# A hybrid Hyena and attention block on one core: plain float32 transforms, contiguous short convolutions, and gate projections placed inside the long convolutions

## The chip, the cores and the metric

The kernel runs on one core of one Trainium2 chip. The core has five engines with a queue of their own each: TensorE (PE; its weight loads are listed as PEld), VectorE (DVE), ScalarE (ACT), GpSimd (POOL) and SyncE (SP, which here only issues DMAs). The metric is the device time of one launch in microseconds. The kernel before took 1945.61 us (median of 3 runs, 1942.84 to 1947.03).

## The reference

One transformer block in float32, 1024 tokens of width 1024, 256 context tokens. A modulated norm of x is projected by one matrix `w_in`. Its first 1536 columns go through the Hyena branch, the next 1536 are queries, keys and values of a differential attention, and the last 2048 are two gates.

```python
h = modulate(rmsnorm(x, g_mix_pre), sh1, sc1)
proj = h @ w_in
y_hy = hyena_branch(proj[..., :1536], ...) @ w_hy_up
...  # rope, diff_attention over own and context keys and values, y_att
g_hy, g_att = split(sigmoid(proj[..., 3072:]), 2)
mixed = (g_hy * y_hy + g_att * y_att) @ w_out
x = x + g1 * rmsnorm(mixed, g_mix_post)
...  # swiglu and its residual

def short_conv(u, w, b):
    up = pad(u, ((0, 0), (1, 1), (0, 0)))
    return up[:, :L] * w[0] + up[:, 1:L + 1] * w[1] + up[:, 2:] * w[2] + b

def fftconv(u, hk, dbias):
    y = irfft(rfft(u, n=2 * L) * hk, n=2 * L)[:, :L]
    return y + u * dbias

def hyena_branch(u, ...):
    parts = split(short_conv(u, conv_w, conv_b), 3)
    z = parts[0]
    for n in range(2):
        z = parts[n + 1] * fftconv(z, hk[:, n], dbias[n])
    return z
```

The filters `hk` are spectra of sequences that a small sine network makes.

## The kernel before

All tiles have 128 partitions. Channels or features lie on partitions, and tokens along a row. One program is written in Python; a tile layer then gives each engine its instructions in an order of its own, by the priority in which they are written and by what its model of the engines says is ready. So the order on an engine is not the order of the text, and it is shown below where it matters. Each engine works strictly in its order.

Float32 products are mostly made as three products in a rounded form (float32r): `whi` times `h_hi`, `wlo` times `h_hi` and `whi` times `h_lo`, where `lo` is what rounding took from `hi`. A rounding is a cast on ACT, the rest a subtraction on DVE.

The stages up to attention:
- **Filters** (`filter_begin` to `filter_end`, four pairs of order `o` and channel half `c`). `make(r)` makes one of eight residues of the filter, `spec(r)` transforms it by products with the matrix `mfs`, and `dft8_even`, `dft8_odd` combine residues on DVE. The spectra go to DRAM (`kspec`). In the same time h is normed and split, and the first tiles of `w_in` are projected (`raw_tile`).
- **A projection tile** (`raw_tile`): load 128 columns of `w_in` (`wraw`), cast (`whi`), subtract (`wlo`), 48 products of 512 columns on PE (two halves of `whi` x8, `wlo` x8, `h_lo` x8), copy to SBUF (`gt`), store to `praw` or `graw`. `wraw`, `whi` and `wlo` have two buffers each.
- **Long convolutions** (`fftconv`, four calls). Forward: per residue pair four transposes on PE, a split (`uh`, `ul`), twelve products with a matrix that is loaded and cast anew each time (`matrix`, tiles `mr`, `mt`), sums from PSUM. Then a chain on DVE: `dft8_even`, product with the spectrum (`times_k`), `dft8_odd`, `times_k`, four sums, and `dft8_even`, `dft8_odd` again. `split` rounds the result (`Hh`, `Hl`); `finish` makes the inverse products, copies (`yt`), transposes back and multiplies into `p`, the other operand of the gate `parts[n + 1]`. The operands `u` and `p` come from `hyena_conv`, the short convolution, which reads and writes with a stride of 8 words, so that residues lie together.
- Around the convolutions `raws` projects the remaining ten tiles of the Hyena part.
- **Gates**: 16 tiles (`graw`), written after the context's statistics (`csq`, `rstd_bc`, `cx`, `c_hi`, `c_lo`), then Q, K and V of head 0, each 48 products, and the context's keys and values (`ctx_k`, `ctx_v`).
- **Attention**, mixing and the feed-forward follow.

Of the kernel before, what the change touches and what calls it, by code (L numbers as in the profile page):

```python
# [9 lines left out]
F32 = mybir.dt.float32  # L10
# [7 lines left out]
P = 128  # L18
# [8 lines left out]
NQUAD, NPAIR, NGEN = 4, 4, 4  # L27
# [4 lines left out]
NMR, NMT = 2, 2  # L32
# [32 lines left out]
def block_kernel(tc, xT, ctxT, cvec, cT, wada1, wada, vecs, lamv, dbias, zT, fw1, fw2, fv, fw3, decay, mfs, mis, rope,  # L65
# [13 lines left out]
    LOENG, M2ENG, HLENG = V, V, V  # L79
# [153 lines left out]
    def dft8_even(S, sign, out):  # L233
        t02, t13 = pair(), pair()
        tt(t02, S[:, 0::2], S[:, 1::2], ALU.add)
        tt(t13, S[:, 0::2], S[:, 1::2], ALU.subtract)
        tt(out[:, 0], t02[:, 0], t02[:, 1], ALU.add)
        tt(out[:, 1], t02[:, 0], t02[:, 1], ALU.subtract)
        pm_i(out[:, 2], t13[:, 0], t13[:, 1], sign)
        pm_i(out[:, 3], t13[:, 0], t13[:, 1], -sign)  # L240

    def dft8_odd(D, sign, out, d3neg=False):
# [24 lines left out]
    mft = fl.tile([P, 4, 1024], F32R, name="mft")  # L267
    mfn = fl.tile([P, 8, 2, P], F32R, name="mfn")
# [77 lines left out]

    def load_mf():
        for r in (0, 2, 1, 3):
            raw = wp.tile([P, 1024], F32, tag="wraw", bufs=2, name="mraw")
            nc.sync.dma_start(out=raw, in_=mfs[r])  # L350
            (A.copy if r % 2 == 0 else G.tensor_copy)(out=mft[:, r], in_=raw)
        for j in range(2):
            m5 = mft.rearrange("p a (j h q m) -> p j a h q m", j=2, h=2, q=2)
            ts(mfn[:, 4 * j:4 * j + 4], f(m5[:, j, :, :, 1]), -1.0, None, ALU.mult, ALU.bypass, G)

    def mfm(part, r):

        if part == 2:
            return mfn[:, r, 0], mfn[:, r, 1]
        c0 = r // 4 * 512 + part * P  # L360
        return mft[:, r % 4, c0:c0 + P], mft[:, r % 4, c0 + 256:c0 + 256 + P]
# [3 lines left out]
    def filter_spec(o, c):  # L365
# [12 lines left out]
        def make(r):  # L378
# [6 lines left out]
            x = fp.tile([P, 512], F32, tag="xb", bufs=2, name="gx")  # L385
# [137 lines left out]
    def hyena_conv(m, dst):  # L523
# [5 lines left out]
        v = lambda k: raw[:, k:k + L].rearrange("p (a r) -> p r a", r=8)  # L529
# [974 lines left out]
```

## Time and profile before

| | |
|---|---|
| runs shown, median | 1945.61 us |
| profiled execution | 1944.66 us, of which its span is 1942.9 us |
| PE busy | 1738.5 us (89% of the span) |
| DVE busy | 1466.7 us (75%) |
| ACT busy | 847.5 us (44%) |
| POOL busy | 72.3 us (4%) |
| mean granted clock of PE | 0.943 of full |
| DMA | 293.95 MB, 151 GB/s over the span |

A busy share is an average over stages with different limits, so the stages are to be read one by one. PE's products are pipelined: the duration of one is longer than the distance from one to the next, and the distance is what counts in a stream. A name such as `ps<-h_hi,whi` gives what an instruction writes and reads.

### The profile page before, as it was taken

The page shows a single profiled execution, that of the slowest core. Times are in us where ns is not written, and L with a number is a line of the kernel's source. Part 1 is how long each engine was busy: PE and PEld are TensorE (multiplying, and loading weights), DVE is VectorE, ACT ScalarE, POOL GpSimd, SP SyncE. Part 2 cuts the span into 40 slices and gives each one's busy share as a digit, 9 for nine tenths or more (in the row PEclk, how much of TensorE's full clock was granted, in tenths as well). Part 3 has the DMA queues.
Part 4 walks back from the last instruction along what each step waited for, and adds up shares of the span by engine and source line. Part 5 has one row for each costly group of instructions (what it writes and reads, how often), then busy time and mean ns, then how long its engine had stood idle before and what let it go on. Part 6 is the DMA issues. An engine that isn't in the chain of part 4 may idle for free.

```text
span 1942.9 us, 23060 instructions
## 1 busy us (share of the span) xinstructions
PE 1738.5 (89%) x8158; PEld 1395.7 (72%) x8158; DVE 1466.7 (75%) x2606; ACT 847.5 (44%) x1306; POOL 72.3 (4%) x72
## 2 busy tenths in 40 slices
PE   7999859567789999999999997889999999798996
PEld 3588647456678888888787775668888888586874
DVE  5898798886946348989885868787776657868667
ACT  4533425334242237666675634453333334444421
POOL 1000000000000121112000000000000000000001
PEclk9899969697989999999999998989999999898998
DMA  9244615234366374443725674322325222434384
GB/s 337 69 171 153 214 58 195 98 129 151 115 251 211 115 218 122 129 135 109 236 90 193 219 241 159 134 85 99 112 104 167 92 76 76 147 104 152 128 302 154
DMA packets 130659, 293.95 MB, mean 151 GB/s; under 512 B 14659, under 2 KB 35919, under 8 KB 129264
## 3 DMA queue, kind: packets, MB, share of 16 engines
q1 hardware_dynamic: 124320, 284.82, 43.1%
q10 hardware_dynamic: 6224, 7.66, 1.3%
q8 instruction: 64, 1.05, 0.2%
q14 instruction: 51, 0.42, 0.1%
HBM read 216.93 MB, written 75.50 MB: 151 GB/s over the span
## 4 chain that ended last, share of the span: by engine, by line
PE 62%; DVE 21%; DMA 8%; ACT 3%; issue 3%; SPq 1%; DVEq 0%; ACTq 0%
PE pj L1151 24%; PE ps L140 22%; DVE pair L83 4%; PE S L840 3%; DVE quad L83 3%; PE psf L408 2%; DVE u L86 2%; PE pt L862 2%; PE psf L614 1%; DMA mr<-mfs 1%; DVE wlo L83 1%; DMA dacc_t<-dacc 1%; PE pv L871 1%; DMA cv<-praw 1%; PE pv L873 1%
## 5 line engine op out<-in xcount | busy, mean ns | idle before, releaser
L83 DVE TENSOR_TENSOR wlo<-wraw,whi 128x512 fp32r<-128x512 f32 (+2 forms) x199 | 167.4, 850 | 94.0 <-ACT whi L132 72.7
L140 PE MATMUL ps<-h_hi,wlo 128*128 128x512 f32 x640 | 179.7, 408 | 3.0 <-DVE wlo L83 3.0
L1151 PE MATMUL pj<-hfc,whi 128*128 128x512 f32 x720 | 178.7, 390 | 0.0
L140 PE MATMUL ps<-h_hi,whi 128*128 128x512 f32 x640 | 171.9, 399 | 3.1 <-ACT h_hi L453 1.9
L140 PE MATMUL ps<-h_lo,whi 128*128 128x512 f32 x640 | 171.4, 394 | 0.0
L1151 PEld LDWEIGHTS pj<-hfc,whi 128*128 128x128 f32 x720 | 135.3, 188 | 28.7
L140 PEld LDWEIGHTS ps<-h_hi,wlo 128*128 128x128 f32 x640 | 121.8, 195 | 27.6 <-DVE wlo L83 4.5
L140 PEld LDWEIGHTS ps<-h_hi,whi 128*128 128x128 f32 x640 | 119.5, 191 | 28.0 <-ACT h_hi L453 3.8
L1151 PE MATMUL pj<-hfb,whi 128*128 128x512 f32 x480 | 127.5, 410 | 11.8 <-ACT whi L1143 11.8
L140 PEld LDWEIGHTS ps<-h_lo,whi 128*128 128x128 f32 x640 | 118.9, 190 | 22.9
L1151 PE MATMUL pj<-hfa,whi 128*128 128x512 f32 x480 | 121.6, 396 | 3.3 <-ACT whi L1143 3.3
L1143 ACT CAST whi<-wraw 128x512 fp32r<-128x512 f32 x120 | 72.4, 621 | 114.3 <-PE pj L1151 84.8
L1151 PEld LDWEIGHTS pj<-hfb,whi 128*128 128x128 f32 x480 | 94.0, 197 | 36.1 <-ACT whi L1143 13.4
L1143 ACT CAST whi<-s 128x512 fp32r<-128x512 f32 x90 | 54.5, 620 | 139.9 <-DVE s L83 89.8
L132 ACT CAST whi<-wraw 128x1024 fp32r<-128x1024 f32 (+2 forms) x94 | 88.2, 940 | 55.3 <-PE ps L140 33.8
L840 PE MATMUL S<-KS,Q 128*128 128x512 f32 (+1 forms) x384 | 107.6, 374 | 2.8 <-DVE pr L844 2.4
L1151 PEld LDWEIGHTS pj<-hfa,whi 128*128 128x128 f32 x480 | 90.8, 190 | 25.2 <-ACT whi L1143 4.4
L1151 PE MATMUL pj<-hfc,wlo 128*128 128x512 f32 x360 | 97.1, 392 | 5.3 <-DVE wlo L83 5.3
L614 PE MATMUL psf<-Hh,mt 128*128 128x256 f32 x128 | 37.2, 389 | 71.8 <-ACT Hh L597 71.8
L501 ACT COPY gt<-ps 128x512 f32<-128x512 f32 x56 | 32.7, 587 | 132.4 <-PE ps L140 88.1
L614 PEld LDWEIGHTS psf<-Hh,mt 128*128 128x128 f32 x128 | 29.3, 280 | 75.5 <-ACT Hh L597 75.2
L1151 PEld LDWEIGHTS pj<-hfc,wlo 128*128 128x128 f32 x360 | 67.3, 188 | 20.9 <-DVE wlo L83 7.0
(486 smaller groups left out, 3803.2 us busy)
## 6 DMA issues: line engine op xcount, KB each, us to landing
wraw<-win SPq DMA_DIRECT2D x46, 512.0 KB, 3.6
wada_t<-wada SPq DMA_DIRECT2D x32, 512.0 KB, 5.4
wraw<-wgate SPq DMA_DIRECT2D x28, 512.0 KB, 3.2
wraw<-wupf SPq DMA_DIRECT2D x28, 512.0 KB, 3.7
araw<-ad SPq DMA_DIRECT2D x44, 256.0 KB, 4.2
w_ada<-wada SPq DMA_DIRECT2D x16, 512.0 KB, 6.3
kspec<-quad SPq DMA_DIRECT2D x8, 1024.0 KB, 3.9
mr<-mfs SPq DMA_DIRECT2D x32, 256.0 KB, 3.7
```

Source lines behind the costliest of these rows:

```text
L83: (eng or V).tensor_tensor(out=out, in0=a, in1=b, op=op)
L86: V.scalar_tensor_tensor(out=out, in0=a, scalar=s, in1=b, op0=op0, op1=op1)
L132: A.copy(out=hi, in_=raw)
L140: T.matmul(out=ps, lhsT=w[:, k * P:(k + 1) * P], rhs=xs[k][j], start=start and i == 0, stop=stop and i == len(seq) - 1)
L408: T.matmul(out=out, lhsT=a, rhs=b, start=i == 0, stop=i == len(ops) - 1)
L501: A.copy(out=gt, in_=ps)
L614: T.matmul(out=po, lhsT=a, rhs=b, start=i == 0, stop=i == len(ops) - 1)
L840: T.matmul(out=S[:, :cn], lhsT=Q[j][:, i, qt * P:(qt + 1) * P], rhs=KS[i][:, c0:c0 + cn], start=j == 0, stop=j == 1)
L862: T.transpose(out=pt[:, b * 256 + qt * P:b * 256 + (qt + 1) * P], in_=av[qt][:, kt * P:(kt + 1) * P], identity=ident)
L871: T.matmul(out=pv[:, :256], lhsT=VH[:, kt], rhs=ah[:, xs], start=kt == 0, stop=False)
L1143: A.copy(out=hi, in_=src)
L1151: T.matmul(out=ps, lhsT=w[a][:, k * P:(k + 1) * P], rhs=xs[k][b], start=i == 0, stop=i == 11)
```

## The change

It has five parts.

1. The transforms by matrices (`spec`, and forward and inverse products in `fftconv`) become plain float32 products, one where there were three. The splits of their operands go (`ghi`, `glo`, `uh`, `ul`, `Hh`, `Hl`). The two halves of the matrices are added up once into `mf` and `mi`, which stay in SBUF; `matrix` and its loads and casts go.
2. The short convolution reads and writes without a stride. The transposes and the product into `p` read with the stride of 8 words in its place; `hyena_out` needs none.
3. The two calls of `pm_i` with opposite signs become one with operands of twice the width.
4. The remaining eight tiles of the Hyena part and the 16 gates' tiles are written inside `fftconv` by `filler`, six in each call. The loop over gates after the context's statistics goes.
5. Buffers: the filter's residues take one buffer of eight; `hk` has 3 buffers, `ut` 2.

```diff
@@ pm_i, dft8_even, dft8_odd
     def pm_i(out, a, b, sign):
-        o1, o2 = (ALU.subtract, ALU.add) if sign > 0 else (ALU.add, ALU.subtract)
-        tt(out[:, RE], a[:, RE], b[:, IM], o1)
-        tt(out[:, IM], a[:, IM], b[:, RE], o2)
+        minus, plus = (ALU.subtract, ALU.add) if sign > 0 else (ALU.add, ALU.subtract)
+        o = out.rearrange("p s (q c) -> p (s q) c", q=2)
+        a2, b2 = [v.rearrange("p (q c) -> p q c", q=2) for v in (a, b)]
+        tt(o[:, 0::3], a2, b2[:, ::-1], minus)
+        tt(o[:, 1:3], a2[:, ::-1], b2, plus)
...
-        pm_i(out[:, 2], t13[:, 0], t13[:, 1], sign)
-        pm_i(out[:, 3], t13[:, 0], t13[:, 1], -sign)
+        pm_i(out[:, 2:4], t13[:, 0], t13[:, 1], sign)
...
+    def matrices(dst, src, tile):
+        d5 = dst.rearrange("p (j r) q m -> p j r (q m)", j=2)
+        for r in (0, 2, 1, 3):
+            raw = tile()
+            nc.sync.dma_start(out=raw, in_=src[r])
+            r4 = raw.rearrange("p (j h x) -> p j h x", j=2, h=2)
+            tt(d5[:, :, r], r4[:, :, 0], r4[:, :, 1], ALU.add)
...
@@ filter_spec
-            hi = fg.tile([P, 512], F32R, tag="ghi", bufs=NGEN, name="ghi")
-            lo = fg.tile([P, 512], F32R, tag="glo", bufs=NGEN, name="glo")
-            A.copy(out=hi, in_=x)
-            tt(lo, x, f(hi), ALU.subtract, LOENG)
-            gen[r] = (hi, lo)
+            gen[r] = x
...
+                T.matmul(out=out, lhsT=mfm(part, r), rhs=gen[r][:, 0:256], start=True, stop=False)
+                T.matmul(out=out, lhsT=mfm(pb, rb), rhs=gen[rb][:, 256:512], start=False, stop=True)
@@ hyena_conv
-        v = lambda k: raw[:, k:k + L].rearrange("p (a r) -> p r a", r=8)
+        v = lambda k: raw[:, k:k + L]
@@ fftconv
-    def fftconv(u, o, c, p):
+    mi = yp.tile([P, 8, 2, P], F32, name="mi")
+    matrices(mi, mis, lambda: yp.tile([P, 1024], F32, tag="hk", bufs=NHK, name="mraw"))
+
+    def fftconv(u, o, c, p, filler):
+        by_r = lambda t: t.rearrange("p h (a r) -> p h r a", r=8)
...
-                    T.transpose(out=pt[:, j * 256 + h * P:j * 256 + (h + 1) * P], in_=u[:, h, rr], identity=ident)
-            uh = yp.tile([P, 512], F32R, tag="uh", bufs=2, name="uh")
-            ul = yp.tile([P, 512], F32R, tag="ul", bufs=2, name="ul")
-            A.copy(out=uh, in_=pt)
-            tt(ul, pt, f(uh), ALU.subtract)
+                    T.transpose(out=pt[:, j * 256 + h * P:j * 256 + (h + 1) * P], in_=by_r(u)[:, h, rr], identity=ident)
+            ut = yp.tile([P, 512], F32, tag="ut", bufs=NUT, name="ut")
+            A.copy(out=ut, in_=pt)
...
-                    T.matmul(out=po, lhsT=mh, rhs=uh[:, xs], start=True, stop=False)
-                    T.matmul(out=po, lhsT=ml, rhs=uh[:, xs], start=False, stop=False)
-                    T.matmul(out=po, lhsT=mh, rhs=ul[:, xs], start=False, stop=True)
+                    T.matmul(out=ps[:, part * 256:(part + 1) * 256], lhsT=mf[:, r + 4 * j, part],
+                             rhs=ut[:, j * 256:(j + 1) * 256], start=True, stop=True)
             sd_from_psum(pp[0], pp[1], S, D_, SLOT[r])
+            if r in (2, 3):
+                filler()
...
         times_k(Ze, 0)
+        filler()
...
         times_k(Zo, 1)
+        filler()
...
-            pv = p[:, :, r:r + 5:4, :]
+            pv = by_r(p)[:, :, r:r + 5:4, :]
             tt(pv, pv, pq.rearrange("p (h j a) -> p h j a", h=2, j=2), ALU.mult)
...
-        finish(0, split(H[:, 0:2]))
-        finish(2, split(H[:, 2:4]))
+        finish(0, [H[:, 0], H[:, 1]])
+        finish(2, [H[:, 2], H[:, 3]])
+        filler()
...
-        finish(3, [h53[1], h17[1]])
+        finish(3, [H[:, 3], H[:, 1]])
+        filler()
...
+    tiles = [(m, praw[m]) for m in (2, 3, 6, 7, 8, 9, 10, 11)] + [(24 + j, graw[j]) for j in range(NGT)]
+
+    def filler():
+        raw_tile(*tiles.pop(0))
...
-    fftconv(u0, 0, 0, p00)
-    raws(2, 3, 6, 7)
+    fftconv(u0, 0, 0, p00, filler)
...
-    for j in range(NGT):
-        raw_tile(24 + j, graw[j])
```

How the orders differ at three places follows. In each row stand the line, the operation, what it writes and reads, the size and how many in a row.

PE in the kernel before, second long convolution, from its last forward product (`ul`, `mt`) to its first inverse ones (`Hh`, `mt`):

```order
L564 MATMUL psf<-ul,mt 128x256
L140 MATMUL ps<-h_hi,whi 128x512 x8
L140 MATMUL ps<-h_hi,wlo 128x512 x8
L140 MATMUL ps<-h_lo,whi 128x512 x8
...
L140 MATMUL ps<-h_hi,whi 128x512 x16
L614 MATMUL psf<-Hh,mt 128x256 x2
L614 MATMUL psf<-Hl,mt 128x256
...
L620 MATMUL psf<-ident,yt 128x128 x4
```

PE in the changed kernel at the same place; `ut`, `mf` are operands of the forward products, `quad`, `mi` of the inverse ones:

```order
L543 MATMUL psf<-ut,mf 128x256 x4
L140 MATMUL ps<-h_hi,wlo 128x512 x8
L140 MATMUL ps<-h_lo,whi 128x512 x8
L140 MATMUL ps<-h_hi,whi 128x512 x8
...
L140 MATMUL ps<-h_hi,whi 128x512 x16
L582 MATMUL psf<-quad,mi 128x256 x4
L589 MATMUL psf<-ident,yt 128x128 x4
L582 MATMUL psf<-quad,mi 128x256 x4
L140 MATMUL ps<-h_hi,wlo 128x512 x4
```

Between the two sets of transform products stand 88 projection products before and 152 now (135 in the first convolution), and more of them stand between the inverse products.

PE in the kernel before, the end of the second Q/K tile, the context's keys (`c_hi`, `c_lo`) and the first V tile; the product `bc` of the context's norm lies some hundred products ahead, among the gates:

```order
L140 MATMUL ps<-h_hi,whi 128x512 x8
L184 MATMUL bc<-dg,ones 128x256
...
L140 MATMUL ps<-h_lo,whi 128x512 x8
L140 MATMUL ps<-c_hi,whi 128x256 x8
L140 MATMUL ps<-c_hi,wlo 128x256 x8
L140 MATMUL ps<-c_lo,whi 128x256 x8
L140 MATMUL ps<-h_hi,whi 128x512 x8
L140 MATMUL ps<-h_hi,wlo 128x512 x8
```

PE in the changed kernel, the second half of the second Q/K tile and what follows it:

```order
L170 MATMUL ss<-ones,csq 128x1 x2
L140 MATMUL ps<-h_hi,whi 128x512 x5
L140 MATMUL ps<-h_hi,wlo 128x512 x8
L140 MATMUL ps<-h_lo,whi 128x512 x8
L184 MATMUL bc<-dg,ones 128x256
L140 MATMUL ps<-c_hi,whi 128x256 x3
L140 MATMUL ps<-h_hi,whi 128x512 x3
...
L140 MATMUL ps<-c_hi,wlo 128x256 x8
L140 MATMUL ps<-c_lo,whi 128x256 x8
L140 MATMUL ps<-h_hi,wlo 128x512 x8
```

The sums of squares and `bc` have moved from among the gates to within and right behind the second Q/K tile, next to the products that need them. From the last row on, the two orders of PE are the same.

DVE in the kernel before, at the end of the small steps that lead to `dg`, the operand of `bc`; `wada_t` is the reduction in `ada_tile`:

```order
L86 SCALAR_TENSOR_TENSOR rs_q<-rs_q,rs 128x2
L83 TENSOR_TENSOR mcol<-vec,cols 128x8
L86 SCALAR_TENSOR_TENSOR rs<-rs_q,rs 128x2
L89 TENSOR_SCALAR dg<-ident,rs 128x128 x2
L151 ISA wada_t,cols<-wada_t,sc_3856,vec 128x1024
L151 ISA cols 128x1
L83 TENSOR_TENSOR cx<-cx,bc 128x2048
```

DVE in the changed kernel, from the shuffle of the second Q/K tile's second half (`sw<-ps`) on:

```order
L712 STREAM_SHUFFLE sw<-ps 128x512
L83 TENSOR_TENSOR rs_q<-rs,rs_m 128x2
L83 TENSOR_TENSOR t_4006<-ps,rp 128x512
L86 SCALAR_TENSOR_TENSOR rs_q<-rs_q,rs 128x2
L83 TENSOR_TENSOR sw<-sw,rp 128x512
L86 SCALAR_TENSOR_TENSOR rs<-rs_q,rs 128x2
L151 ISA wada_t,cols<-wada_t,sc_3796,vec 128x1024
...
L89 TENSOR_SCALAR dg<-ident,rs 128x128 x2
...
L83 TENSOR_TENSOR cx<-cx,bc 128x2048
```

The steps to `dg` now stand among the rope steps of the Q/K tiles, behind a shuffle that reads what PE has just made.

## Rows read from the trace of the kernel before

**Rows 1.** The page: PE and its granted clock in 40 slices, in tenths.
```profile
PE   7999859567789999999999997889999999798996
...
PEclk9899969697989999999999998989999999898998
```

**Rows 2.** Windows: from:to length, PE, PEld, DVE, ACT, POOL busy, clock, DMA.
```profile
79.00:184.00 105.00, 104.34 (x573) 90.62 (x574) 92.92 (x151) 40.38 (x60) 0.00 (x0) 0.96 0.36 128
184.00:233.00 49.00, 39.46 (x190) 31.38 (x189) 36.70 (x42) 23.61 (x28) 0.52 (x8) 0.97 0.68 232
...
320.40:358.50 38.10, 19.99 (x90) 16.21 (x88) 37.44 (x51) 8.74 (x10) 0.00 (x0) 0.81 0.20 70
358.50:406.00 47.50, 38.31 (x192) 31.56 (x193) 33.96 (x39) 26.20 (x37) 0.26 (x4) 0.80 0.58 194
...
556.00:647.50 91.50, 85.27 (x369) 70.01 (x368) 42.16 (x82) 23.96 (x36) 0.00 (x0) 0.96 0.64 229
```

**Rows 3.** Waits of PE, 184 to 648 us: total, times, longest.
```profile
PE psf L614 <- ACT Hh L597: 71.8, 9, 19.1
```

**Rows 4.** Timeline of PE: start, length, line, operation, count [idle before].
```profile
336.57 3.79 PE L140 MATMUL ps<-h_hi,whi 128*128 128x512 f32 x16
358.46 0.80 PE L614 MATMUL psf<-Hh,mt 128*128 128x256 f32 x2 [18.11 <-ACT Hh L597]
```

**Rows 5.** Timeline of PE, a stretch of projections, first and last group.
```profile
645.69 1.98 PE L140 MATMUL ps<-h_lo,whi 128*128 128x512 f32 x8
...
667.45 1.98 PE L140 MATMUL ps<-h_lo,whi 128*128 128x512 f32 x8
```

**Rows 6.** Timeline of PE, split products of 256 columns in a row.
```profile
231.75 0.28 PE L563 MATMUL psf<-uh,mt 128*128 128x256 f32 x1
...
232.94 0.28 PE L564 MATMUL psf<-ul,mt 128*128 128x256 f32 x1
```

**Rows 7.** Plain float32 products: timeline, and line 184 (least, median, most ns).
```profile
59.92 6.17 PE L294 MATMUL ada_ps<-w_ada,csil 128*2 128x512 f32 x14
66.02 1.98 PE L441 MATMUL bc<-dg,ones 128*128 128x512 f32 x4
...
L184 PE MATMUL bc<-dg,ones x14: 379/592/1220, 594.4 to 1930.3; 128*128 128x512 f32 x12, 128*128 128x256 f32 x2
```

**Rows 8.** Groups of DVE, 184 to 560 us: count, busy, mean ns, idle before.
```profile
L86 DVE SCALAR_TENSOR_TENSOR u<-cv,vec,u 128x1024 f32<-128x1024 f32 x24 | 52.4, 2184 | 14.1 <-ACT u L92 8.5 <-issue 5.2
...
L86 DVE SCALAR_TENSOR_TENSOR quad<-pair 128x1024 f32<-128x1024 f32 x18 | 21.2, 1220 | 0.0
...
L83 DVE TENSOR_TENSOR pair<-pair 128x256 f32<-128x256 f32 x36 | 12.8, 420 | 0.0
...
L83 DVE TENSOR_TENSOR u<-u,psf 128x512 f32<-128x512 f32 x16 | 11.0, 688 | 16.7 <-PE psf L620 16.7
```

**Rows 9.** Timeline of DVE, its chain between forward and inverse products: first, last.
```profile
322.27 2.35 DVE L83 TENSOR_TENSOR pair<-quad 128x1024 f32<-128x1024 f32 x2
...
358.60 1.21 DVE L83 TENSOR_TENSOR Hl<-quad,Hh 128x1024 fp32r<-128x1024 f32 x1
```

**Rows 10.** The context's preparation: chain, timelines, a tile's row, PE's first V tile.
```profile
558.78 8.13 DMA zs<-zlo
...
567.01 0.36 ACTq L773 DMA_DIRECT2D cx<-ctxT  x1
...
574.12 1.91 ACT L92 ACTIVATE csq<-cx 128x2048 f32<-128x2048 f32 x1 [5.56 <-DMA cx<-ctxT]
...
L151 DVE CUSTOM_DVE_ANT_0 wada_t<-wada_t,sc,vec x16: 1271/1276/1285, 578.6 to 612.4; 128x1024 f32<-128x1024 f32 x16
...
595.42 2.28 DVE L83 TENSOR_TENSOR cx<-cx,bc 128x2048 f32<-128x2048 f32 x1
...
673.96 1.98 PE L140 MATMUL ps<-h_hi,wlo 128*128 128x512 f32 x8
```

**Rows 11.** Loads of the transposes' stationary operand (least, median, most ns).
```profile
L548 PEld LDWEIGHTS psf<-ident,u x64: 137/140/143, 201.3 to 485.4; 128*128 128x128 f32 x64
```

More of the change, by code (lines that the diff above doesn't have):

```diff
@@ L345, in load_x @@
             nc.sync.dma_start(out=xk[k], in_=xT[k])
-    def load_mf():
[L348 to L354, printed above, removed]
+    def matrices(dst, src, tile):
[5 more added lines that the diff above has]
+            tt(d5[:, :, r], r4[:, :, 0], r4[:, :, 1], ALU.add)
+    def load_mf():
+        matrices(mf, mfs, lambda: wp.tile([P, 1024], F32, tag="wraw", bufs=2, name="mraw"))
+        act(mfn, mf[:, :, 1], AF.Copy, scale=-1.0)
     def mfm(part, r):
[L358 to L361, printed above, removed]
+        return mfn[:, r] if part == 2 else mf[:, r, part]
     fg = fstk.enter_context(pool("fgen", side="right"))
@@ L591, in fftconv @@
         tt(D_[:, 2:4], Zo[:, 0:2], Zo[:, 2:4], ALU.subtract)
-        def split(x):
-            hi = yp.tile([P, 2, 512], F32R, tag="hk", bufs=4, name="Hh")
-            lo = yp.tile([P, 2, 512], F32R, tag="hk", bufs=4, name="Hl")
-            A.copy(out=hi, in_=x)
-            tt(lo, x, f(hi), ALU.subtract, HLENG)
-            return [(hi[:, i], lo[:, i]) for i in range(2)]
         def finish(r, Hs):
@@ L603, in finish @@
             for j in range(2):
-                hi, lo = Hs[j]
-                po = ps[:, j * 256:(j + 1) * 256]
-                ops = []
-                m = matrix(mis[r, :, j * 512:(j + 1) * 512])
                 for part in range(2):
-                    mh = m[:, part * P:(part + 1) * P]
-                    ml = m[:, 256 + part * P:256 + (part + 1) * P]
-                    cs = slice(part * 256, (part + 1) * 256)
-                    ops += [(mh, hi[:, cs]), (ml, hi[:, cs]), (mh, lo[:, cs])]
-                for i, (a, b) in enumerate(ops):
-                    T.matmul(out=po, lhsT=a, rhs=b, start=i == 0, stop=i == len(ops) - 1)
+                    T.matmul(out=ps[:, j * 256:(j + 1) * 256], lhsT=mi[:, r + 4 * j, part],
+                             rhs=Hs[j][:, part * 256:(part + 1) * 256], start=part == 0, stop=part == 1)
             yt = fp.tile([P, 512], F32, tag="xb", bufs=2, name="yt")
@@ L645, in part @@
     def part(o, c):
[L646 removed]
+        p = yp.tile([P, 2, L], F32, tag="u", bufs=3, name="u")
         for h in range(2):
@@ L657, in block_kernel @@
     p00 = part(1, 0)
-    fftconv(u0, 0, 0, p00)
-    raws(2, 3, 6, 7)
+    fftconv(u0, 0, 0, p00, filler)
     u1 = part(0, 1)
     p01 = part(1, 1)
-    fftconv(u1, 0, 1, p01)
-    raws(8, 9, 10, 11)
+    fftconv(u1, 0, 1, p01, filler)
     p10 = part(2, 0)
-    fftconv(p00, 1, 0, p10)
+    fftconv(p00, 1, 0, p10, filler)
     hyena_out(0, p10)
     p11 = part(2, 1)
-    fftconv(p01, 1, 1, p11)
+    fftconv(p01, 1, 1, p11, filler)
     hyena_out(1, p11)
+    while tiles:
+        filler()
     hy.close()
```

53 lines of the change are left out of this document (14 added, 39 removed).

## The prediction

> **What bounds the kernel now.** I began with the page: its forty slices [rows 1] show TensorE (PE) at nine tenths or more nearly everywhere, except in the fifth to twelfth slice (about 195 to 585 us), where it stands at 5 to 9 and the granted clock at 6 to 9 tenths. There lie the long convolutions and the start of the gates' projections. Cutting the span at the stages [rows 2] shows two engines that take turns. Up to 184 us (filters) PE is busy 104.3 of 105.0. Between the last forward product of the second long convolution (320.4) and its first inverse one (358.5) VectorE (DVE) is busy 37.4 of 38.1 and PE 20.0. From there to 406 PE has 38.3 of 47.5 and DVE 34.0, at a granted clock of 0.80. In the gates (556 to 647.5) PE has 85.3 of 91.5 and DVE 42.2. The waits say on what PE stands: 71.8 us in nine waits for `Hh`, the rounded result of DVE's transform [rows 3]. In the timeline [rows 4] it runs out of projections after `whi` x16 at 336.57 and starts the inverse products 18.11 us after those end. So the stage is bound by DVE's chain, and the gates by PE, one after the other.
>
> **The change, part by part.** From the second group of products of the first V tile on (`wlo` x8 in `v_tile(0)`) PE's order is word for word the same in both programs. Before reaches it at 673.96 [rows 10]; the sum is the time at which the changed program does.
>
> Prices. A split product of 512 columns: 12 groups of 8 from 645.69 to 667.45, 0.227 us each [rows 5]. One of 256 columns: ten from 231.75 to 232.94, 0.119 [rows 6]. A plain float32 product leaves two records, since the two calls of L441 left four. Fourteen records of 512 columns take 6.10 us, 0.436 each, and one of 256 columns is 0.213 shorter (379 against 592 ns) [rows 7]; that makes 0.223 per record, 0.45 per product. Bounds: 0.43 (twice 0.213), and 0.56, if I take the four records in 1.98 us at 66.02 (0.495 each) and subtract the same. I take 0.45, since fourteen in a row resemble the new stream most. So three split products (0.36) become one of 0.45: on PE the plain transform is dearer, by 256 x 0.09 = 24 us. What the change can give is waiting, not work.
>
> DVE loses, per convolution, four `ul` (0.69 each) and four `Hl` (1.22), as other ops of their width. Each short convolution's two steps fall from 2.18 to 1.22, their operands being contiguous now. The merged sums save 4 x 0.42 - 2 x 0.69 = 0.3 us each at most [rows 8]. ScalarE (ACT) loses the casts of both matrices and of `Hh`. It was under 60% busy in these stages and ends no long chain but that of `Hh`, whose cast of 1.05 goes. SP loses a matrix load per product group.
>
> Segment A, to the last filter product (184.0 before). Three filters: 96 x 0.45 - 288 x 0.119 = +9; the first filter +3, of which 2 beyond its DMA gaps. The scheduler places 140 projection products ahead of that point, not 230: -20.4. I add 1.4 for waits that those had filled: 176. DVE, busy 92.9 of 105.0 [rows 2] and now 24 x 0.69 us lighter, does not take over.
>
> Segment B, to the last forward product of the first convolution (48.9 us before). The first operand is ready after the last sums from PSUM (2.3 us), DVE's last filter transform (four ops of 1024 at 1.14, which two in a row show as 2.35 [rows 9], ten of 512 at 0.6: 10.6), four sums for the inverse matrices (2.4), two `wlo` (2.3), four short-convolution steps (4.6) and a wait for the `cv` load between them (one buffer; I take 2.6 of 0 to 5): 25 us. The four forward steps take 15: 40. PE's work there (125 products of a tile, 16 plain ones, 16 transposes) is 37, so 37 and the old 49 are the bounds.
>
> Segment C, three periods, from one convolution's last forward product to the next one's. PE's work: six tiles of 48 x 0.227 = 65.3, 32 plain products 14.5, 32 transposes of 0.09: 82.7. DVE's chain to the first inverse product was 36.3 us [rows 9]. Now a `wlo` of 1.14 stands where a short-convolution step of 2.18 stood, four sums are merged and the cast is gone: 36.1 from the last forward product, where PE has 152 x 0.227 = 34.4 of projections (first convolution: 135, 30.6). It waits 1.7 us (5.5), not 18.1; waits for `yt` and `ut` add 2.5. 86.5 each, three: 260. (Before: 85, but with four tiles.) Every filler brings a load on SP behind `cv` and `kk` loads, a cast on ACT and a `wlo` of 1.22 on DVE. The ring has two `wlo`, so DVE waits for PE's tile before last; in the order that binds once a convolution, for 5 us behind the last tile, with only short convolutions queued behind it.
>
> Segment D, from the last forward product of the fourth convolution. Gap and inverse part, through the last gate tile: 64. Two Q/K tiles: 22, together 86. Here the gates had been the cover of the context's preparation, and it is gone. From the last `zlo` (about 61) the load of `cx` can be issued 8 us later, as before (558.8 to 567.0), and its squares start 7 us after that [rows 10]. Then DVE stands in order: the small steps of `rstd` come after the fourth `STREAM_SHUFFLE`, which waits for PE at 86, and between them are three 1.28 us `wada` reductions and rope steps. `dg` is ready at 97, the product with it at 98, `cx` scaled after two more reductions and 2.28 at 102, the last `c_lo` at 110. PE stands at `bc` and at the first `c_hi` for some 20 us, then needs 5 us of work, and 2 for a clock that falls in it: 113 in place of 91. If nothing were late, 91; if the loads of `wada` and `rope` crowd `cx`, 125.
>
> Sum: 176 + 40 + 260 + 113 = 589, against 673.96: -85. The profiled execution took 1944.66 (span 1942.9 and 1.8 around it), so **1860**. The median of the runs shown is 1945.61, 0.95 above it; I leave that.
>
> A rule weighed. Short-convolution steps with a stride of 8 words took 2.18, contiguous ones 1.22 [rows 8]; the change moves this stride to the transposes' stationary loads (0.14 now [rows 11]) and to `u<-u,psf`. The Trainium skill, "SBUF — State Buffer", section "Door 1: The DMA port swizzle", says that reads which leave a 16-byte line with each element lose bandwidth, for whichever engine reads. The trace agrees for DVE; for PE's loads no run here shows it. By the rule the sum would be 1869, by DVE's row alone 1860.
>
> **Rivals.**
> - Strided stationary loads take twice as long and are not hidden: 64 x 0.14 = 9 us, **1869**. For it: the same stride nearly doubles a DVE step. Against: loads run beside products. (This is the rule above.)
> - The fillers tie PE and DVE together: a `wlo` waits for PE, transforms queue behind it, PE waits for them. Price 10 us a convolution, **1900**. For it: DVE in order, a ring of two. Against: by the count above each `wlo` finds its buffer free but one.
> - The fillers land elsewhere than in the waits: four waits of 18 stay in place of 2.7 each, **1921**. Against: the order shows 152 products ahead of the inverse ones where 88 stood.
> - The context is ready in time (no wait in segment D): **1840**.
> - The other side: a plain product costs twice what I take, because its two weight loads can't hide behind 256 columns. 224 products on the path x 0.45 = +101: **1961**, slower. It decides from 0.45 + 85/224 = 0.83 us per product. Against: even the four slowest records give 0.56.
>
> **How the numbers follow.** Forecast 0.55, strided loads 0.08, tied engines 0.17, fillers elsewhere 0.05, context in time 0.12, dear product 0.03. The forecast's own range is 1846 to 1884: products at 0.43 or 0.56 are -5 or +25, segment B -3 or +9. The range of 1838 to 1905 leaves out the fillers elsewhere and the dear product. A change under 0.2% (3.9 us) can't be told from none; only the dear product ends beyond it on the slow side, so faster 0.96, same 0.01, slower 0.03.
>
> **What would show it.** Right: PE busy over 90% in every stretch from 180 to 545 us, granted clock near 1.0 there, PE's wait for the inverse products' operand under 6 us each, last filter product near 176, the four convolutions 86 us apart, `wlo` of the first V tile near 589, and before it one PE wait of about 10 us on `dg`. Wrong: plain products more than 0.5 us apart, PE waiting on `wlo` with DVE waiting on PE, or a period near 95.

## The result and the profile after

The changed kernel took 1858.97 us (median of 4 runs, 1857.21 to 1860.01), the kernel before beside it 1944.22. The ratio is 0.9565, with a 95% interval of 0.9541 to 0.9589. The forecast was 1860. The profiled execution took 1857.21, its span 1855.4.

The page's slices of PE and its granted clock, to be held against [rows 1]:

```profile
PE   7999989999997999999999987989999999798995
...
PEclk9899999999998999999999988999999999898998
```

The dip from the fifth slice on is gone. A short one stays in the thirteenth (557 to 603 us). The windows say more: the stretch from the last filter product to the last forward product of the first convolution, three periods from one convolution's last forward product to the next one's, and the rest up to `wlo` x8 of the first V tile (columns as in [rows 2]):

```profile
167.00:208.00 41.00, 38.03 (x174) 30.78 (x173) 31.53 (x37) 15.12 (x22) 0.40 (x6) 1.00 0.76 269
208.00:297.00 89.00, 82.93 (x367) 67.54 (x366) 66.88 (x75) 24.48 (x34) 0.66 (x10) 0.96 0.37 121
297.00:383.00 86.00, 83.60 (x386) 68.69 (x384) 60.87 (x71) 21.75 (x32) 0.27 (x4) 1.00 0.33 110
383.00:468.00 85.00, 82.59 (x380) 67.79 (x379) 62.68 (x72) 22.61 (x33) 0.13 (x2) 1.00 0.38 126
468.00:581.50 113.50, 96.56 (x423) 78.77 (x422) 91.69 (x144) 27.32 (x40) 5.85 (x4) 0.91 0.54 185
```

PE is busy 83.6 of 86.0 in a convolution that now holds six projection tiles. Before, two engines took turns [rows 2]; now PE alone is the bound until 530 us. What PE still waits for, from 80 to 620 us (total, times, longest):

```profile
PE psf L582 <- DVE quad L83: 8.4, 4, 4.3
PE bc L184 <- DVE dg L89: 8.1, 1, 8.1
PE ps L140 <- ACT c_hi L759: 5.4, 1, 5.4
```

The first row answers to [rows 3]: 71.8 us in nine waits became 8.4 in four. The other two are the new ones, in the tail. The timeline of PE around the second convolution's first inverse products, and the common point:

```profile
327.74 3.79 PE L140 MATMUL ps<-h_hi,whi 128*128 128x512 f32 x16
333.25 1.97 PE L582 MATMUL psf<-quad,mi 128*128 128x256 f32 x8 [1.73 <-DVE quad L83]
...
581.46 2.00 PE L140 MATMUL ps<-h_hi,wlo 128*128 128x512 f32 x8
```

At the same place [rows 4] had 18.11 us of waiting. The common point comes at 581.46 in place of 673.96 [rows 10]: 92.5 us earlier. The rest of the program takes 1273.9 us after it, 5.0 more than before; PE is busy as long there (1188.1 and 1188.3), so these are waits.

Where the 92.5 went is told by PE's busy time up to that point. Windows of the kernel before, then of the changed one, split at the last filter product:

```profile
0.00:184.30 184.30, 169.50 (x819) 121.32 (x820) 143.79 (x248) 74.37 (x102) 9.70 (x12) 0.94 0.49 177
184.30:673.96 489.66, 380.68 (x1761) 311.59 (x1761) 363.21 (x489) 178.49 (x236) 6.48 (x28) 0.87 0.45 156
```

```profile
0.00:166.60 166.60, 153.47 (x601) 104.52 (x602) 120.98 (x200) 50.00 (x63) 1.79 (x8) 0.97 0.51 183
166.60:581.46 414.86, 384.07 (x1723) 313.85 (x1721) 313.62 (x396) 111.65 (x160) 7.45 (x28) 0.97 0.45 152
```

Without work PE was 123.8 us before and 43.9 now: 79.9 of the 92.5. Busy time fell by 12.6, though the plain products are dearer: 256 x (0.431 - 0.357) = 19. So some 32 us less went into the same other work, and the granted clock goes with that (0.87 against 0.97 in the second stretch). A wait was paid twice, once as idle time and once as slow products behind it.

### The profile page after: what moved, and what is told of

It is laid out like the page before. It is cut to its first block, busy times and chain, and to the rows that moved or that the text cites. A ratio compares the mean times of both kernels' runs of the same rounds, so it can differ in the third digit from the quotient of the medians.

```text
span 1855.4 us, 22179 instructions
## 1 busy us (share of the span) xinstructions
PE 1725.7 (93%) x7902; PEld 1379.9 (74%) x7902; DVE 1400.7 (75%) x2478; ACT 757.0 (41%) x1193; POOL 65.2 (4%) x68
## 4 chain that ended last, share of the span: by engine, by line
PE 64%; DVE 21%; DMA 8%; issue 3%; ACT 2%; SPq 0%; DVEq 0%; ACTq 0%
PE pj L1121 27%; PE ps L140 19%; DVE pair L83 4%; PE S L810 4%; DVE quad L83 3%; DVE wlo L83 2%; PE pt L832 2%; PE psf L398 2%; PE psf L399 2%; PE psf L582 1%; DMA dacc_t<-dacc 1%; PE psf L543 1%; PE pv L841 1%; DMA wada_t<-wada 1%; PE psf L384 1%
## 5 line engine op out<-in xcount | busy, mean ns | idle before, releaser
L140 PE MATMUL ps<-h_hi,wlo 128*128 128x512 f32 x640 | 173.9, 401 | 0.7 <-DVE wlo L83 0.7
L140 PE MATMUL ps<-h_lo,whi 128*128 128x512 f32 x640 | 166.8, 393 | 0.0
L1121 PEld LDWEIGHTS pj<-hfb,whi 128*128 128x128 f32 x480 | 94.0, 197 | 36.2 <-ACT whi L1113 13.4
L1121 PEld LDWEIGHTS pj<-hfa,whi 128*128 128x128 f32 x480 | 89.6, 188 | 26.8 <-ACT whi L1113 6.7
L83 DVE TENSOR_TENSOR wlo<-s,whi 128x512 fp32r<-128x512 f32 x90 | 60.1, 686 | 27.3 <-PE pj L1121 27.3
L810 PEld LDWEIGHTS S<-KS,Q 128*128 128x128 f32 x384 | 64.4, 189 | 17.7 <-DVE pr L814 9.4
```

The costliest lines, as they stand in the source:

```text
L83: (eng or V).tensor_tensor(out=out, in0=a, in1=b, op=op)
L140: T.matmul(out=ps, lhsT=w[:, k * P:(k + 1) * P], rhs=xs[k][j], start=start and i == 0, stop=stop and i == len(seq) - 1)
L810: T.matmul(out=S[:, :cn], lhsT=Q[j][:, i, qt * P:(qt + 1) * P], rhs=KS[i][:, c0:c0 + cn], start=j == 0, stop=j == 1)
L1121: T.matmul(out=ps, lhsT=w[a][:, k * P:(k + 1) * P], rhs=xs[k][b], start=i == 0, stop=i == 11)
```

## The experiments

Each kernel was profiled and timed beside the kernel before. The table splits the profiled executions as the forecast did: A up to the last filter product, B to the last forward product of the first convolution, C the three periods, D to the common point, then the rest of the span.

| kernel | A | B | C | D | rest | median us | ratio (95%) |
|---|---|---|---|---|---|---|---|
| before | 184.3 | 48.9 | 257.7 | 183.1 | 1268.9 | 1944.22 | 1 |
| changed | 166.6 | 41.1 | 261.8 | 111.9 | 1273.9 | 1858.97 | 0.9565 (0.9541 to 0.9589) |
| fillers only | 181.2 | 47.3 | 277.6 | 117.4 | 1271.2 | 1898.72 | 0.9774 (0.9752 to 0.9797) |
| no fillers | 170.0 | 43.5 | 199.4 | 203.8 | 1276.5 | 1898.78 | 0.9767 (0.9746 to 0.9787) |
| split transforms | 187.0 | 40.4 | 261.4 | 112.8 | 1272.0 | 1873.73 | 0.9639 (0.9618 to 0.9660) |
| strided | 167.4 | 48.5 | 284.0 | 111.0 | 1272.5 | 1885.33 | 0.9700 (0.9680 to 0.9721) |
| unmerged | 169.5 | 41.0 | 269.2 | 111.3 | 1275.3 | 1867.35 | 0.9603 (0.9580 to 0.9625) |

Part A varies by 5 us among kernels that are the same there (166.3 to 171.1, the kernels of experiments 6 to 8 taken in), so single differences of that size mean nothing.

**1. Fillers only.** The kernel before, with the tiles written by `filler` inside `fftconv`:

```diff
         times_k(Ze, 0)
+        filler()
...
-    for j in range(NGT):
-        raw_tile(24 + j, graw[j])
```

> Kernel before with one part of the change only: the eight raw and sixteen gate tiles are written inside the long convolutions; the transforms stay split (float32r), short convolutions strided, sums unmerged. Theory 1 (most of the gain is waits that projections now fill): last filter product at 184 as before, convolutions about 89 us apart with a PE wait for Hh of 5 to 7 us each in place of 18, context wait at the tail as in the changed kernel; 1889 us. Rival (the gain comes from DVE's shorter work in the plain transforms, and fillers in front of a split chain only tie PE and DVE together): waits of over 10 us for Hh or for wlo remain, 1920 us or more.

Measured 1898.72, between the two. PE's waits for the inverse products' operand fell from 71.8 to 23.2 us, 3.8 to 6.5 at the first inverse products of each convolution and one of 3.2 more:

```profile
PE psf L618 <- ACT Hh L601: 23.2, 5, 6.5
PE bc L184 <- DVE dg L89: 8.1, 1, 8.1
PE ps L140 <- DVE wlo L83: 7.7, 2, 5.6
```

The waits came out nearly as theory 1 had them; the convolutions were longer than it said (92.5 us in place of 89), with 7.7 us for `wlo` that it had not. The longer of these two waits, PE's timeline and DVE's:

```profile
252.73 3.78 PE L140 MATMUL ps<-h_hi,wlo 128*128 128x512 f32 x8 [5.65 <-DVE wlo L83]
```

```profile
251.46 1.22 DVE L83 TENSOR_TENSOR wlo<-wraw,whi 128x1024 fp32r<-128x1024 f32 x1
```

That much of the rival is true: PE can stand at a `wlo` that is queued within DVE's chain. Its loop is not shown, since DVE worked without a pause from 230.4 us until then and waited for nothing of PE's.

**2. No fillers.** The changed kernel with the tiles back between the convolutions and behind the context's statistics:

```diff
-        filler()
...
+    raws(2, 3, 6, 7)
...
+    for j in range(NGT):
+        raw_tile(24 + j, graw[j])
```

> Changed kernel without the fillers: raw tiles between the convolutions and gates behind the context's statistics, as before; plain transforms, contiguous short convolutions and merged sums stay. Theory 1: PE has 135, 134, 75 and 124 projections between forward and inverse products, against a DVE chain of about 36 us: waits of 4, 6, 19 and 8 us there, some 5 us more per convolution ahead of the odd residues' inverse products, and in return no wait for the context; 1905 us (1890 to 1920). Rival (the transforms and the lighter DVE carry the gain, the fillers only move work): 1865 us or less.

Measured 1898.78, within theory 1's range. The four waits for the inverse products, one row of PE's timeline each:

```profile
248.57 1.84 PE L578 MATMUL psf<-quad,mi 128*128 128x256 f32 x5 [4.36 <-DVE quad L83]
...
321.28 2.07 PE L578 MATMUL psf<-quad,mi 128*128 128x256 f32 x4 [4.54 <-DVE quad L83]
...
385.84 1.65 PE L578 MATMUL psf<-quad,mi 128*128 128x256 f32 x3 [19.14 <-DVE quad L83]
...
447.96 1.65 PE L578 MATMUL psf<-quad,mi 128*128 128x256 f32 x3 [5.46 <-DVE quad L83]
```

Expected were 4, 6, 19 and 8. So a wait here is DVE's chain (36 us) less the projections that stand in front (135, 134, 75, 124 of 0.227 us), and the order alone foretells it. Fillers alone give 46 us, the other parts alone 46; together 85, nearly the sum.

**3. Split transforms.** Part 1 undone, everything else kept (three float32r products, `uh`, `ul`, `Hh`, `Hl`, `matrix` and their buffers as before):

```diff
-                    T.matmul(out=ps[:, part * 256:(part + 1) * 256], lhsT=mf[:, r + 4 * j, part],
-                             rhs=ut[:, j * 256:(j + 1) * 256], start=True, stop=True)
+                    T.matmul(out=po, lhsT=mh, rhs=uh[:, xs], start=True, stop=False)
+                    T.matmul(out=po, lhsT=ml, rhs=uh[:, xs], start=False, stop=False)
+                    T.matmul(out=po, lhsT=mh, rhs=ul[:, xs], start=False, stop=True)
```

> Changed kernel with the transforms back in split form (three float32r products, splits on ACT and DVE, matrices loaded and cast each time, buffers as before); fillers, contiguous short convolutions and merged sums stay. Theory 1: last filter product back near 182 (166 in the changed kernel), the convolutions' period 88 us (PE has 2.4 us less of work in each, but waits some 5 us longer for Hh): 1880 us. Rival (PE is now the bound everywhere, so what counts is PE's work: three split products 0.36 against one plain 0.43): some 9 us less in the filters and 10 in the convolutions, 1840 us.

Measured 1873.73; theory 1 stands, 6 us off. Part A is 20.4 us longer. That is the price of the 90 projections that the order puts there (230 against 140), but the split products are some 9 us cheaper there, so about as much went into waits and slower products. B to D take the same time with 90 projections less to do. Up to the common point PE's busy time is the same in both kernels (536.3 and 537.5), and without work it is 65.4 us here and 43.9 in the changed kernel. So the plain form is worth its 15 us by less waiting (24.4 us for `Hh` here, 8.4 for `quad` in its place), and PE's dearer products are paid out of that. The rival's 1840 is out: PE's own work was 19 us less, and it was not what counted.

**4. Strided short convolution.** Part 2 undone:

```diff
-        v = lambda k: raw[:, k:k + L]
+        v = lambda k: raw[:, k:k + L].rearrange("p (a r) -> p r a", r=8)
...
-            pv = by_r(p)[:, :, r:r + 5:4, :]
+            pv = p[:, :, r:r + 5:4, :]
```

> Changed kernel with the short convolution strided again (so the stationary loads of the forward transposes and the product into p are contiguous). Theory 1: short-convolution steps cost DVE 0.96 us more each, which shows ahead of the first convolution (about 4 us) and in the last z (about 4 us), hidden elsewhere behind PE: 1864 us. Rival (strided stationary loads are what PE now pays for, 64 loads): forward transposes get faster, up to 9 us off, and the DVE steps are hidden: 1850 us.

Measured 1885.33: both theories failed. DVE's steps were to be hidden in C, and C grew by 22; B, which theory 1 had 4 us longer, grew by 7. The timeline of DVE at the head of its chain in the second convolution, here and (second fence) in the changed kernel:

```profile
315.95 4.53 DVE L86 SCALAR_TENSOR_TENSOR u<-cv,vec,u 128x1024 f32<-128x1024 f32 x2 [1.40 <-issue]
320.41 1.27 DVE L83 TENSOR_TENSOR quad<-psf,xb 128x512 f32<-128x512 f32 x2
```

```profile
296.22 2.67 DVE L86 SCALAR_TENSOR_TENSOR u<-cv,vec,u 128x1024 f32<-128x1024 f32 x2 [0.39 <-issue]
298.81 1.28 DVE L83 TENSOR_TENSOR quad<-psf,xb 128x512 f32<-128x512 f32 x2
```

Two steps of the next short convolution stand ahead of the last sums, in the chain that PE waits for (the buffer for the next `u` comes free with the last transposes). They are 1.9 us longer here, and ACT's own step ahead of them is 1.0 longer (2.26 in place of 1.25; the idle time in the bracket is that much more). So from PE's last forward product to its first inverse one it takes 39.5 us in place of 36.6, and 2.0 of these 2.9 come out as more waiting (3.74 in place of 1.73). Then the clock fell. Windows of this kernel around that wait (clock in the third column from the right):

```profile
351.00:355.00 4.00, 0.26 (x2) 0.19 (x2) 4.00 (x5) 0.00 (x0) 0.00 (x0) 1.00 0.00 0
355.00:357.00 2.00, 2.00 (x7) 1.58 (x7) 2.00 (x4) 0.00 (x0) 0.00 (x0) 0.61 0.00 0
357.00:359.00 2.00, 1.32 (x5) 0.60 (x4) 1.24 (x2) 0.59 (x1) 0.00 (x0) 0.50 0.13 27
359.00:361.00 2.00, 2.00 (x8) 1.73 (x7) 1.14 (x2) 0.00 (x0) 0.00 (x0) 0.50 0.63 236
```

0.50 is the lower of the two levels, 1.2 GHz. The eight records of the first inverse products took 3.19 us here and 1.97 in the changed kernel, whose clock stayed at 1.00 there. In all this period grew from 86.3 to 92.1, and so did the next. In six kernels of experiments 6 to 8, whose program is the changed kernel's in this part, the second period was 86.2 to 86.3, so its length there is no chance of one execution. The first grew by 10.5: there the copy `ut` stands on ACT behind a short-convolution step that waits for its `cv` load, and the one `cv` buffer comes free only behind DVE's longer steps; PE waited 7.3 us for that `ut` (1.5 in the changed kernel).

The stationary loads did get dearer by the stride (all 64, least, median, most ns): 140 in this kernel, 188 in the changed one.

```profile
L535 PEld LDWEIGHTS psf<-ident,u x64: 138/140/143, 186.5 to 496.8; 128*128 128x128 f32 x64
```

```profile
L536 PEld LDWEIGHTS psf<-ident,u x64: 185/188/206, 184.0 to 466.4; 128*128 128x128 f32 x64
```

But four transposes in a row hold PE for 0.36 us in the changed kernel and 0.35 here. The Trainium skill's rule ("SBUF — State Buffer", section "Door 1: The DMA port swizzle") holds for PE's loads too, then, with 48 ns in place of the 140 that the rival took, and none of it shows.

**5. Unmerged sums.** Part 3 undone:

```diff
-        pm_i(out[:, 2:4], t13[:, 0], t13[:, 1], sign)
+        pm_i(out[:, 2], t13[:, 0], t13[:, 1], sign)
+        pm_i(out[:, 3], t13[:, 0], t13[:, 1], -sign)
```

> Changed kernel with the two separate calls of pm_i again (four sums of 0.42 us in place of two of 0.69). Theory 1: DVE's chain between forward and inverse products gets 1.2 us longer (even, odd, even), which PE's wait there shows one for one, and where the wait passes from 1.7 to about 3 us the granted clock falls behind it, as with the strided short convolution (about 3 us more): +4 us in each of two to three convolutions, 1869 us. Rival (waits just add up, the clock plays no part): +1.2 each, 1863 us; second rival (hidden behind PE): 1859 us.

Measured 1867.35 (+8.4), near theory 1; the interval (0.9580 to 0.9625) does not exclude the first rival's 1863, so the trace has to decide. The chain was priced too long: its separate sums cost 0.42 us more in all, not 1.2, and the wait went from 1.73 to 2.15. PE's timeline and windows in the second convolution:

```profile
338.43 3.07 PE L583 MATMUL psf<-quad,mi 128*128 128x256 f32 x8 [2.15 <-DVE quad L83]
```

```profile
336.00:338.40 2.40, 0.28 (x2) 0.01 (x1) 2.40 (x4) 0.00 (x0) 0.00 (x0) 1.00 0.00 0
338.40:340.00 1.60, 1.57 (x5) 1.34 (x6) 1.60 (x5) 0.00 (x0) 0.00 (x0) 0.73 0.00 0
340.00:342.00 2.00, 1.50 (x4) 0.67 (x2) 1.96 (x3) 0.47 (x1) 0.00 (x0) 0.50 0.00 0
342.00:344.00 2.00, 1.83 (x7) 1.65 (x8) 0.67 (x1) 0.12 (x1) 0.00 (x0) 0.50 0.69 238
344.00:346.00 2.00, 2.00 (x6) 1.62 (x5) 2.00 (x6) 0.00 (x0) 0.00 (x0) 0.51 0.06 25
```

So 0.42 us on the chain cost this period 3.3 (89.6 in place of 86.3). The third convolution did the same (a wait of 2.14 us, then 0.50). In the first the clock stayed at 1.00 behind a wait of 2.98, and in the strided kernel behind waits of 2.49 and 2.56, so the length of the wait alone does not decide. That first convolution lost its time elsewhere: PE had stood 4.55 us at a `wlo` in DVE's chain before, and there the clock fell to 0.50. Part A is 2.9 us longer too, which is within what A varies by.

**6. The tail.** D held 16 us of new waits. Three kernels gave it other cover: the last two gate tiles behind the context's statistics, the V tile ahead of the context's keys, and both.

```diff
+    HOLD = 2
...
-        raw_tile(*tiles.pop(0))
+        if len(tiles) > HOLD:
+            raw_tile(*tiles.pop(0))
...
+    for t in tiles:
+        raw_tile(*t)
     qk_tile(12, [qs[0][0], qs[1][0]])
-    qk_tile(16, [ks[0][0], ks[1][0]], ctx_k)
-    v_tile(0, ctx_v)
+    qk_tile(16, [ks[0][0], ks[1][0]], lambda hd, a, b: kw.append((a, b)))
+    v_tile(0, lambda hd, a, b: vw.append((a, b)))
+    ctx_k(0, *kw[0])
+    ctx_v(0, *vw[0])
```

> Changed kernel with the last two gate tiles written behind the context's statistics instead of inside the last convolution (the same work on every engine). Theory 1: what the tail lost is order, not work: on DVE the steps to dg and the scaling of cx now stand ahead of the fourth shuffle and most of the wada reductions, and PE has 51 projections between the sums of squares and bc in place of 21: the waits for dg (8.1), c_hi (5.3) and most of the gaps among the context's products go: 16 us less, 1843 us. Rival (the context is late because its load and DVE's chain are long, wherever the tiles stand; and the inverse part of the last convolution loses its cover): within 4 us of the changed kernel, 1855 to 1862 us.

> Changed kernel with the first V tile's 48 projections written ahead of the context's keys, all gate tiles where the changed kernel has them. Theory 1: 11 us of PE work now stand between the second Q/K tile and the context's products: waits for dg and c_hi shrink by that much, 1847 us. Rival (DVE in order keeps dg and c_hi equally far behind PE, since V's splits queue there as well): 1857 us.

> Both edits of the two kernels beside it: the last two gate tiles behind the context's statistics, and the V tile ahead of the context's keys. Theory 1: the first edit alone removes the waits, the second finds nothing left: 1843 us, the same as the first alone. Rival (some 4 us of waits among the context's products stay with the first alone): 1839 us.

Measured 1864.49 (0.9595, 0.9572 to 0.9618), 1854.55 (0.9543, 0.9517 to 0.9569) and 1868.56 (0.9615, 0.9582 to 0.9647). Theory 1 fell for the first and third, and so did the third's rival. The context's squares start at the same time wherever the gate tiles stand; ACT's timeline with two tiles held back, then of the changed kernel:

```profile
545.76 1.91 ACT L92 ACTIVATE csq<-cx 128x2048 f32<-128x2048 f32 x1 [7.43 <-DMA cx<-ctxT]
```

```profile
545.67 1.92 ACT L92 ACTIVATE csq<-cx 128x2048 f32<-128x2048 f32 x1 [4.10 <-DMA cx<-ctxT]
```

So the rival comes nearer there: the load sets the start, and DVE's steps up to the scaled `cx` the end. With two tiles held back PE waited no more at `bc`, but still 5.0 us at `c_hi`, and 4.7 at the sums of squares (2.2 in the changed kernel). The V tile as cover did remove most of the two waits, which are 8.1 and 5.4 in the changed kernel (waits of PE, 80 to 620 us):

```profile
PE bc L184 <- DVE dg L89: 1.7, 1, 1.7
...
PE ps L140 <- ACT c_hi L759: 0.8, 1, 0.8
```

From the last forward product of the fourth convolution to the end of the span that kernel took 1377.4 us. D and the rest make 1385.8 in the changed kernel, and 1383.5 to 1388.6 in the five of the table that have fillers. So theory 1 had the mechanism; ahead of that point this execution was 3.2 us longer, which is within what part A varies by. By the medians the edit is worth 4 us, and its interval overlaps with the changed kernel's, so a gain is not shown.

**7. Statistics early.** `ctxT` loaded once more into a free buffer of `u`, its squares, sums and the diagonal made in the last convolution (first kernel) or ahead of it (second); the third adds a tile to the first convolution.

```diff
+    cxe = yp.tile([P, 2, L], F32, tag="u", bufs=3, name="cxe").rearrange("p h (k t) -> p (h k) t", t=C)
+    nc.scalar.dma_start(out=cxe, in_=ctxT)
+    csq = quad("csq").rearrange("p a (k t) -> p (a k) t", t=C)
+    act(csq, cxe, AF.Square)
...
-    bc = rstd_bc(pa, csq[:, 0], C, D, xp, "tr", NTR)
+    bc = diag_bc(pa, dgc, C, "tr", NTR)
```

> Changed kernel with the context's statistics early: ctxT is loaded once more into a free buffer during the last long convolution, squared and summed there, and the diagonal of rstd made before that convolution's z is out; behind it only the second load, the product with bc and the scaling remain. The kernel that held two gate tiles back showed that the tail waits for the context's load (landed at 545.7 in both) and then for 14 us of small steps that queue on DVE among rope steps. Theory 1: with these steps gone from behind the load, c_hi is ready some 12 us earlier, PE has 85 projections ahead of it, and the tail loses its 16 us of waits: 1844 us. Rival (the load alone is late enough: DVE stands at cx with the splits of the next Q/K tile queued behind it, so PE waits for wlo instead): 1855 us.

> The same, with the statistics one step earlier: ahead of the last convolution's forward sums. Theory 1: as the kernel beside it, 1844 us, if the early load has landed when DVE comes to its sums. Rival: DVE waits there for the load with the forward sums behind it, and the fourth convolution is some 5 us longer: 1850 us.

> Early statistics, and one more gate tile between the forward and inverse products of the first convolution (167 projections there in place of 135; the last convolution has one tile less behind its inverse products). Theory 1: the first convolution's wait of 4.3 us and the low clock behind it (about 3 us) go as well, and the tail has cover enough without that tile: 1838 us. Rival (the tile is missed in the tail: PE comes to the context 7 us earlier and waits there): 1845 us, no better than the early statistics alone.

Measured 1854.14 (0.9532, 0.9499 to 0.9565), 1858.37 (0.9547, 0.9524 to 0.9570) and 1865.26 (0.9582, 0.9554 to 0.9609). In the first D fell to 102.4, but PE met a new wait. DVE's and PE's rows:

```profile
548.46 2.29 DVE L83 TENSOR_TENSOR cx<-cx,bc 128x2048 f32<-128x2048 f32 x1 [3.42 <-DMA cx<-ctxT]
```

```profile
556.95 2.08 PE L140 MATMUL ps<-h_hi,whi 128*128 128x512 f32 x4 [8.14 <-DVE t L83]
```

DVE stands at `cx` for its load, the rope step that frees PE's accumulator is queued behind the scaling, and PE waits for that: the rival's way, with `t` in `wlo`'s place. Of the 9.5 us saved in D, 5.8 are lost again behind the common point. In the second kernel neither figure was met: the last period grew by 2.6 us, PE waited 4.4 for `t`, and 5.4 behind the common point for a `whi`. In the third the wait ahead of the first inverse products did go (0 in place of 4.3), and the kernel was slower than its rival had it: that tile was missing later (PE waited 2.8 at `bc` and 3.8 at `c_hi`), and 7.8 more went behind the common point at a `whi` whose load of `w_in` came late, which no text had foretold.

**8. The rest of the context on POOL.** The first kernel of 7, with product, scaling and `c_lo` on POOL:

```diff
-    tt(cx, cx, bc[:, :C].unsqueeze(1).broadcast_to([P, KD, C]), ALU.mult)
+    A.copy(out=bcs_, in_=bc[:, :C])
+    tt(cx, cx, bcs_.unsqueeze(1).broadcast_to([P, KD, C]), ALU.mult, G)
...
-        ts(cx[:, k], cx[:, k], mcol[:, 8 + k:9 + k], cols[:, 48 + k:49 + k], ALU.mult, ALU.add)
+        ts(cx[:, k], cx[:, k], mcol[:, 8 + k:9 + k], cols[:, 48 + k:49 + k], ALU.mult, ALU.add, G)
...
-        tt(c_lo[:, k], cx[:, k], f(c_hi[:, k]), ALU.subtract)
+        tt(c_lo[:, k], cx[:, k], f(c_hi[:, k]), ALU.subtract, G)
```

> The kernel with the early statistics, and the rest of the context's preparation (product with bc, scaling, c_lo) moved from DVE to POOL, so that nothing of it stands in DVE's order. There PE lost 8.1 us on a rope step that queued on DVE behind the product with cx, which stood there for the load of cx (landed at 548.5). Theory 1 (what is left of the tail's loss is DVE's order): that wait goes; POOL takes 2.5 ns per column (2.6 us for 1024 in the changed kernel), so some 15 us for all three steps, and PE has 85 projections (19 us) over them: some 4 us of waiting at c_lo remain, 1850 us. Rival (POOL and DVE hinder each other, or the time comes back in attention, as the 11 us of the early statistics mostly did): 1854 to 1858 us.

Measured 1859.16 (0.9550, 0.9527 to 0.9573), at the rival's upper end. POOL's and DVE's timelines:

```profile
552.47 5.30 POOL L83 TENSOR_TENSOR cx<-cx,bcs__3829 128x2048 f32<-128x2048 f32 x1 [161.94 <-DMA wada_t<-wada]
...
567.14 5.53 POOL L83 TENSOR_TENSOR c_lo<-cx,c_hi 128x256 fp32r<-128x256 f32 x8
```

```profile
553.23 5.10 DVE L83 TENSOR_TENSOR t<-t,sw 128x512 f32<-128x512 f32 x1
...
569.11 5.88 DVE L83 TENSOR_TENSOR wlo<-wraw,whi 128x1024 fp32r<-128x1024 f32 x1 [3.97 <-ACT whi L132]
```

The bracket is idle time before the step, and what ended it. A step of 0.69 us took 5.10 and ended 0.6 behind POOL's product; one of 1.22 took 5.88 and ended 2.3 behind the eight subtractions, which another step of POOL had followed at once. The Trainium skill says so ("SBUF — State Buffer", section "Who interferes with whom": DVE and GpSimd share a port pair under an exclusive lock); the trace agrees for these steps, and not beside POOL's scaling, where a DVE step of 0.68 us with two operands in SBUF took 0.89. PE stood 5.05 us at `t` again, since its rope step was queued behind that `wlo`.

No version beat the changed kernel by more than the intervals; the two lowest medians are 1854.14 and 1854.55.

## Why the prediction was right

The forecast was 1860, measured 1858.97, and the mechanism is the one it gave: projections in DVE's chain took 18 us waits down to 1.7. By its steps:

- **Segment A** (to 176) failed on the size: 166.6. The second filter's first product came at 77.5, not 2 or 3 us later than before (81.8) but 4.3 earlier (78.7 and 80.5 in two kernels that are the same there): from 20 to 52 us PE was busy 32.0 of 32.0 (28.4 before, at a clock of 0.89), without the waits for rounded operands that stood there before. A plain product took 0.431, the lower bound, not 0.45 (96 x 0.019 = 1.8 us). The 1.4 us added for waits were not there.
- **Segment B** (40): 41.1. **Segment C** (260): 261.8, with periods of 89.3, 86.3 and 86.2; the waits were 4.3, 1.7, 1.7 where 5.5 and 1.7 had stood. The working's own terms do not give its 260: 82.7 and 2.5 with the waits named make 90.7 and twice 86.9, so 264.5, and the forecast would have been 1864. Nor does the forecast's own range of 1846 to 1884 follow from the terms named for it, which give 1852 to 1894.
- **Segment D** (113): 111.9. PE stood 8.1 us at `bc` and 5.4 at the first `c_hi`, less than the 20 written, and was through the two Q/K tiles 3.5 us later than written, with a wait of 2.2 at the sums of squares. `dg` was made at 567, 97 us after the last forward product, as written.
- **Behind the common point** the sum took no change, and 5.0 us were lost there. The other kernels lose 2 to 8 there. Why stays open. With A's 9.4 us too many, this is why 1860 came out so close: two errors of opposite sign, which is luck.
- **The rivals.** Strided loads: loads dearer by 48 ns, hidden. Tied engines: not in the changed kernel (0.7 us for `wlo`). PE stood 7.7 us at `wlo` with fillers only, but 5.6 in the unmerged kernel with its plain transforms and 2.1 in the split one, so the form of the transforms does not decide it; and in the longest of these waits no `wlo` waited for PE, as the rival's loop needs. Fillers elsewhere, context in time, dear product: no.
- **What the working missed**: the contiguous short convolution was priced as hidden but for B, and is worth 26 us; the merged sums were priced at 0.3 us each, and undoing them cost 8. Both shorten a chain at whose end PE waits just little enough for the clock to stay. The forecast took the chain's length right (36.1, measured 36.2) but said that the short-convolution steps had left it; they stand at its head.

## What to carry to other kernels

Where two engines take turns, compare the chain of the one with the work of the other that the order puts beside it: chain less cover gave each wait within 3 us here, before the run and for kernels with other orders. When the cover nearly equals the chain, tenths of a microsecond on the chain count for several, since PE may fall to its lower clock behind the wait. And to remove a wait in the tail is not yet to gain its time: of seven attempts, one (the V tile ahead) took most of it out and shortened the tail, the others met the next wait, of DVE's order or of a late load, and none beat the changed kernel beyond its interval.

## What the runs showed that was not expected

- The granted clock stayed at 1.00 behind PE's waits of 1.73 us and fell to 0.50 for some 4 to 7 us behind 2.14, 2.15, 3.74 and 4.30; yet it stayed behind 2.49, 2.56 and 2.98 at other places.
- A plain float32 product of 256 columns starts every 0.431 us, in two records of 0.216, also where 4 follow each other with new weights each.
- DVE steps with two operands in SBUF stood still for 4 to 5 us beside POOL's product and subtractions. Beside POOL's scaling by columns (eight steps of 0.98) DVE's steps lost 0.2 us at most.
